# One factor of the short convolution: from two column products to a seven-product block behind the other factor's

## The chip, the cores and the metric

The kernel runs on one core of one Trainium2 chip. The metric is the device time of one execution in microseconds (us), as the median of several runs. TensorE (PE in the profile, its weight loads PEld) multiplies, VectorE (DVE) and ScalarE (ACT) work elementwise, GpSimd (POOL) and SyncE (SP) here mostly issue DMAs.

## What is computed

One decoder layer on 256 tokens of width 2048, all in float32: half a SwiGLU feed-forward, a token mixer, half a second feed-forward, a final norm. The mixer's part of the reference, where all five pieces come from one projection `w_in` (2048 x 5120):

```python
z = rms_norm(x, mix_norm[l]) @ w_in[l]
# lru_x, lru_gate, sc_b, sc_c, sc_x: 1024 columns of z each
xc = causal_depthwise_conv(lru_x, lru_conv_w[l]) + lru_conv_b[l]
h = rg_lru(xc, lru_w_a[l], lru_b_a[l], lru_w_i[l], lru_b_i[l], lru_lambda[l])
y_lru = h * jax.nn.gelu(lru_gate, approximate=True)
y_sc = sc_b * causal_depthwise_conv(sc_c * sc_x, sc_conv_w[l])
y = jnp.concatenate([rms_norm(y_lru, lru_out_norm[l]), rms_norm(y_sc, sc_out_norm[l])], axis=-1)
x = x + y @ w_out[l]
```

The text calls `sc_c` C and `sc_x` X. They are only needed as their product.

## The kernel before

Every float32 operand is split into a high part (float32r, "hi") and a low part (the rest, "lo"); hi x hi, hi x lo and lo x hi are summed in PSUM. A weight tile of 512 rows x 512 columns, a *unit*, is loaded by SP as 1 MB (`raw`), cast by ScalarE in two halves (`hi`), and its low part made by VectorE (raw minus hi). A pair of hi and lo buffers is reused when TensorE has used it; outside the blocks there are two pairs and three rooms for raw.

The input projection has two forms. `columns` makes 512 columns of z, transposed (columns on the partitions): four units, each with 16 matmuls of a 128 x 128 weight piece against 512 elements (hi and lo of x side by side) and 16 against 256. Its result comes in two halves that ScalarE copies and VectorE adds. After each unit `pump` takes deferred work from a queue until a budget is used up, and it is by `defer` that the convolutions, gates, scans and GELUs of the eight heads are spread over the following units.

`seven` makes 1024 columns at once, with tokens on the partitions, as 2 x 2 blocks: of the 16 products of 512 rows, 512 columns and 128 tokens, the 8 over rows 0 to 1023 become 7 products of sums (Strassen's scheme), so 15 remain, each of 12 matmuls against 512 elements. The four weight blocks of rows 0 to 1023 are `w11`, `w12`, `w21`, `w22`; those of the rest are `b2`, `b3`, `a2`, `a3`. The order of the work is: product 0 (on w11), product 4 (on w11 + w12), b2 twice, product 5 (w22 added), b3 twice, product 6 (w12 + w22), product 2 (w22), a2 twice, product 3 (on w11 + w21, with w11 as the earlier sums left it), a3 twice, product 1 (w21). The sums are VectorE's, made in place in w11, except `w12 += w22`, which is a DMA that accumulates, issued by POOL. `w11` and `w12` lie in rooms of their own, the other six take turns in the three raw rooms, so w21 is loaded where w22 was. Inputs of products are named `_p`, the plain ones `_x`. Snapshots of PSUM (`snap`) are combined in `done`, and `turn` transposes the finished 512 columns back.

Before, only C was made by `seven` (in `sc_c`, between the first and the second call of `columns`); X by two calls of `columns` (`sc_x`) among seven: lru_x 1, gate 0, X 0, gate 1, X 1, b 0, b 1. After them comes the output projection (`product`, tiles `o`), whose rows 0 to 1023 are the eight heads (`yT`).

A scheduler orders the instructions of each engine when the program is built, by the order in which the code is written and by when it takes operands to be ready. At run time each engine goes through its list in order, and so do POOL's and SP's queues.

Of the kernel before, what the change touches and what calls it, by code (L numbers as in the profile page):

```python
# [176 lines left out]
def hybrid_block(ctx: ExitStack, tc: tile.TileContext, a: dict, out: bass.AP):  # L177
# [10 lines left out]
    def defer(cost, fn):  # L188
        pending.append((cost, fn))
# [437 lines left out]
    def whole(u):  # L627
        return [(UK * u, UK)]
# [4 lines left out]
    def quad(tile):  # L633
        return tile.rearrange("p (j c) -> p j c", j=UK)

    def seven(w, rows, cols, sf, xs, name, keep, done, between=None, early=False, own=None, factor=None):

# [1117 lines left out]
    with ExitStack() as mixer:  # L1755
# [128 lines left out]
        def lru_x(ps, half):  # L1884
            qs = range(4 * half, 4 * half + 4)
            for f, q in enumerate(qs):
                z = tmp("zx", q, S + 3, bufs=4)
                nc.gpsimd.memset(z[:, :3], 0.0)
                b = halves(ps[f], f"x{q}")
                dve.tensor_tensor(b, ps[f][:, :S], b, op=ALU.add)  # L1890
                dve.tensor_tensor(z[:, 3:], b, bc, op=ALU.mult)
                zx[q] = z
            ts[half] = tmp("T", half, 4 * S)
            for q in qs:
                hs[q] = ts[half][:, (q % 4) * S : (q % 4 + 1) * S]
                defer(1.2, lambda q=q: conv_lru(q))
                defer(0.8, lambda q=q: gates(q))
            defer(3.1, lambda: inverse(half))
            defer(2.8, lambda: drive(half))
            for q in qs:  # L1900
                defer(0.6, lambda q=q: scan(q))

        def lru_gate(ps, half):
            for f in range(4):
# [26 lines left out]
            last()  # L1931
            part(2)

        def sc_c(between):
            r2 = work.tile([P, NT], F32, tag="r2", name="r2")
            dve.tensor_tensor(r2, nm.r, nm.r, op=ALU.mult)
            rt = [r2[:, t : t + 1] for t in range(NT)]
            r2n = work.tile([P, NT], F32, tag="r2n", name="r2n")
            dve.tensor_scalar(r2n, r2, -1.0, None, op0=ALU.mult)
            nt = [r2n[:, t : t + 1] for t in range(NT)]  # L1940
            room = [tmp(tag, "snap", 4 * S, bufs=1) for tag in "vd"]
            free = [b[:, o : o + CW] for b in room for o in (0, CW)]
            z = {}

            def turn(n):
                for f in range(0, 4, 2):
                    pt = bank(f"pt_c{n}_{f}")
                    for i in range(2):
                        for t in range(NT):
                            o = i * S + t * P  # L1950
                            pe.transpose(pt[:, o : o + P], z[t, n][:, (f + i) * P : (f + i + 1) * P], ident)
                    for i in range(2):
                        q = 4 * (1 - n) + f + i
                        c = tmp("cc", q, S + 2, bufs=8)
                        nc.gpsimd.memset(c[:, :2], 0.0)
                        act.copy(c[:, 2:], pt[:, i * S : (i + 1) * S])
                        cc[q] = c

            def done(t, n, ps, tiles):
                for p in tiles[1:]:  # L1960
                    dve.tensor_tensor(tiles[0], tiles[0], p, op=ALU.add)
                    free.append(p)
                if tiles:
                    z[t, n] = tiles[0]
                    dve.scalar_tensor_tensor(z[t, n], ps, rt[t], z[t, n], op0=ALU.mult, op1=ALU.add)
                else:
                    z[t, n] = free.pop()
                    act.activation(z[t, n], ps, AF.Copy, scale=rt[t])
                if (t, n) == (1, 0):
                    turn(1)  # L1970

            c0 = 3 * (D // 2)
            extra.append(bigs)
            turn_of["split"] = 0
            seven(
                w_in, (whole(0), whole(1)), (c0 + CW, c0), si, [of_unit(u, nm.xT[u]) for u in (2, 3)], "in_c", lambda name: free.pop(0), done,
                lambda i: between() if i == 1 else None,
                factor={"s1": rt[0], "s5": rt[1], "u2": nt[0], "u3": nt[1]},
            )
# [12 lines left out]
        def sc_b(ps, half):  # L1992
            if any(4 * half + f not in ys for f in range(4)):
# [7 lines left out]
                defer(0.8, lambda q=q, y=y: finish(y, NH + q, vec["sc_out_norm"][:, q : q + 1], 1, q == 0))  # L2001

        order = [
            (lru_x, 0, 0), (lru_x, 0, 1), (lru_gate, 1, 0), (sc_x, 4, 0), (lru_gate, 1, 1), (sc_x, 4, 1),
            (sc_b, 2, 0), (sc_b, 2, 1),
        ]
        operands()
        behind = None
        for i, (use, part, half) in enumerate(order):
            ps = columns(w_in, part * (D // 2) + half * CW, nm.xT, f"in_{part}_{half}", behind)  # L2010
            behind = None
            if i == 0:
# [5 lines left out]
                behind = sc_c(lambda: use(ps, half))  # L2018
# [196 lines left out]
```

## Time and profile before

| | |
|---|---|
| median of 3 runs | 1715.32 us (1714.56 to 1715.74) |
| the profiled execution | 1716.32 us, of which its span (first to last instruction) is 1714.5 |
| granted TensorE clock | 0.999 |
| input projection in the span | 698.3 to 927.8 us |
| block of C | 723.0 to 764.9 us |
| output projection | 927.8 us onwards |

A timeline row gives the start, the duration, the engine, the line, the operation, out<-in, the shapes and how many alike follow each other; behind it, in brackets, idle time of the engine before it and what ended it. Most rows say L43, the line of a helper, so tiles tell them apart. A windows row gives the stretch, its length, and for PE, PEld, DVE, ACT and POOL the busy time with the number of instructions, then the granted clock, the share of DMA time and GB/s. A group row ends with busy us and mean ns of one, and the idle time before. A waits row gives us in total, times, and the longest.

### The profile page before, as it was taken

Reading aid. Unit: us, or ns where it says so; the run is one execution under the profiler, and the core shown is the slowest. Engines: PE = TensorE matmul, PEld = TensorE weight load, DVE = VectorE, ACT = ScalarE, POOL = GpSimd, SP = SyncE. Lnnn points to the kernel's source line nnn. Section 1 sums busy time; section 2 is a strip of 40 time slices with the busy share of each in tenths; the row PEclk is TensorE's granted clock in tenths of the full one; section 3 lists DMA queues with packets and bytes.
Section 4 is the critical chain, followed back from the end, with each engine's and each line's share of the span. In section 5 each row is a group of like instructions: output and inputs, shape, how many; then the busy total and the mean of one; then the engine's idle time right before and its main releaser. Section 6 shows DMA issues by size and latency. Waiting matters only on the chain.

```text
span 1714.5 us, 20422 instructions
## 1 busy us (share of the span) xinstructions
PE 1701.4 (99%) x7889; PEld 1416.4 (83%) x7889; DVE 1549.2 (90%) x1346; ACT 1109.7 (65%) x1360; POOL 56.0 (3%) x90
## 2 busy tenths in 40 slices
PE   9999999999999999999999999999999999999997
PEld 8888888888888888888888888888888888888886
DVE  7989999999899998887897888899899998999997
ACT  7666576665666667667865666656666665666665
POOL 0010000000000000000000000000000000000000
PEclk9999999999999999999999999999999999999999
DMA  8776877769877768755556674675777878877774
GB/s 283 235 220 197 263 246 227 232 212 265 284 227 227 258 199 255 245 175 180 175 195 206 210 259 148 220 243 173 233 251 233 266 239 243 270 226 240 230 245 148
DMA packets 183315, 389.39 MB, mean 227 GB/s; under 512 B 7605, under 2 KB 10545, under 8 KB 177969
## 3 DMA queue, kind: packets, MB, share of 16 engines
q1 hardware_dynamic: 174656, 340.81, 56.8%
q0 software_dynamic: 8384, 46.21, 13.9%
q8 instruction: 62, 1.02, 0.2%
q10 hardware_dynamic: 176, 1.06, 0.2%
q14 instruction: 37, 0.30, 0.0%
HBM read 339.82 MB, written 2.10 MB: 199 GB/s over the span
## 4 chain that ended last, share of the span: by engine, by line
PE 96%; DVE 2%; ACT 1%; issue 0%; DMA 0%; DVEq 0%; ACTq 0%
PE ps_in L43 10%; PE ps_g_a L43 10%; PE ps_u_a L43 10%; PE ps_d_a L43 9%; PE ps_g_c L43 6%; PE ps_u_c L43 6%; PE ps_d_c L43 5%; PE ps_g_d L43 4%; PE ps_u_d L43 4%; PE ps_d_d L43 4%; PE ps_d_e L43 4%; PE ps_d L43 4%; PE ps_o L43 3%; PE ps_g_e L43 3%; PE ps_u_e L43 2%; PE ps_g L43 2%
## 5 line engine op out<-in xcount | busy, mean ns | idle before, releaser
L43 ACT CAST hi_g_p<-raw_g_w 128x1024 fp32r<-128x1024 f32 (+1 forms) x112 | 139.2, 1263 | 97.4 <-DVE raw_g_w L43 34.5
L43 ACT CAST hi_u_p<-raw_u_w 128x1024 fp32r<-128x1024 f32 x112 | 138.2, 1262 | 66.5 <-PE ps_u_a L43 19.1
L43 DVE TENSOR_TENSOR lo_g_p<-raw_g_w,hi_g_p 128x2560 fp32r<-128x2560 f32 (+2 forms) x72 | 159.9, 2228 | 15.7 <-ACT hi_g_p L43 8.8
L43 DVE TENSOR_TENSOR lo_u_p<-raw_u_w,hi_u_p 128x2560 fp32r<-128x2560 f32 (+2 forms) x72 | 159.1, 2228 | 9.4 <-ACT hi_u_p L43 6.7
L43 ACT CAST hi_d_p<-raw_d_w 128x1024 fp32r<-128x1024 f32 x112 | 112.7, 1047 | 53.7 <-DVE raw_d_w L43 22.3
L43 DVE TENSOR_TENSOR lo_d_p<-raw_d_w,hi_d_p 128x2048 fp32r<-128x2048 f32 (+1 forms) x72 | 129.4, 1812 | 5.8 <-ACT hi_d_p L43 5.5
L43 PE MATMUL ps_in<-xT_nm,hi_in 128*128 128x512 f32 x512 | 123.5, 392 | 0.0
L43 PEld LDWEIGHTS ps_in<-xT_nm,hi_in 128*128 128x128 f32 x512 | 94.0, 188 | 18.7 <-ACT tha L43 0.5
L43 DVE TENSOR_TENSOR lo_in<-raw_in,hi_in 128x2048 fp32r<-128x2048 f32 x32 | 73.3, 2291 | 20.4 <-ACT hi_in L43 20.0
L43 ACT CAST hi_in<-raw_in 128x1024 fp32r<-128x1024 f32 x64 | 64.0, 1045 | 32.2 <-PE ps_in L43 18.4
L43 ACT CAST hi_d_x<-raw_d_x 128x1024 fp32r<-128x1024 f32 x64 | 64.3, 1046 | 19.3 <-PE ps_d_c L43 8.1
L43 DVE TENSOR_TENSOR lo_d_x<-raw_d_x,hi_d_x 128x2048 fp32r<-128x2048 f32 x32 | 72.7, 2286 | 1.5 <-ACT hi_d_x L43 1.3
L43 DVE TENSOR_TENSOR raw_u_w<-raw_u_w,raw_u_w 128x1024 f32<-128x1024 f32 (+2 forms) x40 | 69.4, 1757 | 3.8 <-DMA raw_u_w<-in_ffn_w_up_dram 3.0
L43 DVE TENSOR_TENSOR raw_g_w<-raw_g_w,raw_g_w 128x1024 f32<-128x1024 f32 (+2 forms) x40 | 69.5, 1755 | 1.4 <-DMA raw_g_w<-in_ffn_w_gate_dram 0.8
L43 PEld LDWEIGHTS ps_in<-xT_nm,lo_in 128*128 128x128 f32 x512 | 65.6, 191 | 2.5
L43 PE MATMUL ps_in<-xT_nm,lo_in 128*128 128x256 f32 x512 | 66.4, 283 | 0.0
L43 DVE TENSOR_TENSOR lo_g_x<-raw_g_x,hi_g_x 128x1536 fp32r<-128x1536 f32 x32 | 56.1, 1754 | 3.7 <-ACT hi_g_x L43 3.6
L43 PE MATMUL ps_u_a<-hi_u_p,x 128*128 128x512 f32 x224 | 57.1, 391 | 0.0
L43 ACT CAST hi_g_x<-raw_g_x 128x1536 fp32r<-128x1536 f32 x32 | 47.2, 1475 | 15.1 <-DMA raw_g_x<-in_ffn_w_gate_dram 11.3
L43 PE MATMUL ps_g_a<-hi_g_p,x 128*128 128x512 f32 x224 | 56.6, 389 | 0.0
L43 DVE TENSOR_TENSOR lo_u_x<-raw_u_x,hi_u_x 128x1536 fp32r<-128x1536 f32 x32 | 56.1, 1753 | 0.0
L43 ACT CAST hi_u_x<-raw_u_x 128x1536 fp32r<-128x1536 f32 x32 | 47.3, 1477 | 12.4 <-PE ps_u_c L43 7.0
(513 smaller groups left out, 4248.1 us busy)
## 6 DMA issues: line engine op xcount, KB each, us to landing
raw_g_w<-in_ffn_w_gate_dram SPq DMA_DIRECT2D x32, 1024.0 KB, 6.6
raw_u_w<-in_ffn_w_up_dram SPq DMA_DIRECT2D x32, 1024.0 KB, 6.4
raw_d_w<-in_ffn_w_down_dram SPq DMA_DIRECT2D x32, 1024.0 KB, 5.4
raw_d_x<-in_ffn_w_down_dram SPq DMA_DIRECT2D x32, 1024.0 KB, 6.9
raw_in<-in_w_in_dram SPq DMA_DIRECT2D x32, 1024.0 KB, 5.0
raw_d<-in_ffn_w_down_dram SPq DMA_DIRECT2D x24, 1024.0 KB, 5.2
raw_g_x<-in_ffn_w_gate_dram SPq DMA_DIRECT2D x32, 768.0 KB, 7.8
raw_u_x<-in_ffn_w_up_dram SPq DMA_DIRECT2D x32, 768.0 KB, 8.5
```

The costliest lines, as they stand in the source:

```text
L43: ins = getattr(self.engine, name)(*args, **kwargs)
```

## The change

X is made by `seven` too, right behind C: `sc_c` becomes `token_block`, called for C and then for X by `sc_cx`. C's last transposes are written behind X's first product, and X's transposed columns are multiplied into C's (`times_x`) straight from PSUM. In both blocks `w11 += w21` becomes an accumulating DMA of POOL (`moved=True`). The two calls of `columns` for X go, the budget of `pump` in `columns` goes from 1.9 to 2.9, and the short convolution of the second four column tiles is deferred by `lru_x`.

```diff
-            pump(1.9)
+            pump(2.9)
...
         product_of(0, w11, a, True)
+        if moved:
+            between("first product")
         dve.tensor_tensor(w11, w12, w11, op=ALU.add)
         nc.gpsimd.dma_start(w12, w22, accum_op=ALU.add)
...
         product_of(5, w11, a)
+        if moved:
+            nc.gpsimd.dma_start(w11, w21, accum_op=ALU.add)
...
-        dve.tensor_tensor(w11, w21, w11, op=ALU.add)
+        if not moved:
+            dve.tensor_tensor(w11, w21, w11, op=ALU.add)
         product_of(3, w11, a, end=own is not None or not two)
...
             for q in qs:
                 defer(0.6, lambda q=q: scan(q))
+            for q in qs if half else ():
+                defer(1.5, lambda q=q: conv_short(q))
...
-        def sc_x(ps, half):
-            for f in range(4):
-                q = 4 * half + f
...
+            def times_x(q, pt):
                 c = cc[q][:, 2:]
-                b = halves(ps[f], f"sx{q}")
-                dve.tensor_tensor(b, ps[f][:, :S], b, op=ALU.add)
-                dve.tensor_tensor(c, b, c, op=ALU.mult)
-                defer(1.5, lambda q=q: conv_short(q))
+                dve.tensor_tensor(c, pt, c, op=ALU.mult)
+                if q < 4:
+                    defer(1.5, lambda: conv_short(q))
+
+            rest = token_block(3, "in_c", lambda i: between() if i == 1 else None, as_c, (rt, nt))
+            return token_block(4, "in_x", lambda i: rest() if i == "first product" else None, times_x)
...
         order = [
-            (lru_x, 0, 0), (lru_x, 0, 1), (lru_gate, 1, 0), (sc_x, 4, 0), (lru_gate, 1, 1), (sc_x, 4, 1),
-            (sc_b, 2, 0), (sc_b, 2, 1),
+            (lru_x, 0, 0), (lru_x, 0, 1), (lru_gate, 1, 0), (lru_gate, 1, 1), (sc_b, 2, 0), (sc_b, 2, 1),
         ]
```

How this moves instructions, in the order in which each engine has them. Numbers in names are the program's own; brackets name the semaphores that are waited for (DMASW: a DMA of POOL, DMAHW: one of SP).

First, VectorE at the end of the block of C, before (here 5631 is w11, 5643 is w21, `lo_in_c_p_5856` is product 3's low part, `lo_in_c_p_5925` product 1's):

```order
L43 TENSOR_TENSOR d_snap<-d_snap,v_snap 128x512 [waits Activation_49]
L43 TENSOR_TENSOR raw_in_c_5631<-raw_in_c_5643,raw_in_c_5631 128x2048 [waits DMAHW2_49]
L43 SCALAR_TENSOR_TENSOR d_snap<-ps_in_c_e,r_5621,d_snap 128x512 [waits DVE_49]
L43 SCALAR_TENSOR_TENSOR d_snap<-ps_in_c_c,r_5621,d_snap 128x512 [waits PE_49]
L43 TENSOR_TENSOR lo_in_c_x_5873<-raw_in_c_5645,hi_in_c_x_5872 128x2048 [waits DMAHW1_49,Activation_49]
L43 TENSOR_TENSOR lo_in_c_p_5856<-raw_in_c_5631,hi_in_c_p_5855 128x2048 [waits DVE_49,Activation_49]
L43 TENSOR_TENSOR lo_in_c_p_5925<-raw_in_c_5643,hi_in_c_p_5924 128x2048 [waits PE_49,Activation_49]
```

and in the changed program:

```order
L43 TENSOR_TENSOR d_snap_in_c<-d_snap_in_c,v_snap_in_c 128x512 [waits Activation_49]
L43 SCALAR_TENSOR_TENSOR xc_6406<-zx_5726,cols_conv,xc_6406 128x256 [waits DVE_49]
L43 SCALAR_TENSOR_TENSOR d_snap_in_c<-ps_in_c_e,r_5621,d_snap_in_c 128x512 [waits DVE_49]
L43 SCALAR_TENSOR_TENSOR xc_6406<-zx_5726,cols_conv,xc_6406 128x256 [waits DVE_49]
L43 SCALAR_TENSOR_TENSOR d_snap_in_c<-ps_in_c_c,r_5621,d_snap_in_c 128x512 [waits PE_49]
L43 TENSOR_TENSOR lo_in_c_x_5873<-raw_in_c_5645,hi_in_c_x_5872 128x2048 [waits DMAHW1_49,Activation_49]
L43 TENSOR_TENSOR lo_in_c_p_5856<-raw_in_c_5631,hi_in_c_p_5855 128x2048 [waits DMASW6_49,Activation_49]
L43 TENSOR_TENSOR lo_in_c_p_5925<-raw_in_c_5643,hi_in_c_p_5924 128x2048 [waits DMAHW2_49,PE_49,Activation_49]
```

The sum `raw_in_c_5631<-raw_in_c_5643,raw_in_c_5631` is gone from VectorE, product 3's low part waits for a DMA of POOL instead, two rows of a head's convolution (`xc_6406`) have moved in, and X's first low part follows directly.

Second, POOL's queue from the accumulating DMA of C on (`zx` are the padded inputs of the heads' convolutions, `raw_o_q` belongs to the output projection), before:

```order
L682 DMA raw_in_c_5633<-raw_in_c_5637 128x2048 [waits DMAHW6_49,DMAHW4_49,DVE_49]
L1888 MEMSET zx_6232 128x3 [waits DVE_49,Activation_49]
L1888 MEMSET zx_6238 128x3 [waits DVE_49,Activation_49]
L1888 MEMSET zx_6244 128x3 [waits DVE_49,Activation_49]
L1888 MEMSET zx_6250 128x3 [waits DVE_49,Activation_49]
L682 DMA raw_o_q_8008<-raw_o_q_8012 128x2048 [waits DMAHW1_49,DMASW4_49,DMAHW3_49,DVE_49,Activation_49]
```

and in the changed program:

```order
L684 DMA raw_in_c_5633<-raw_in_c_5637 128x2048 [waits DMAHW6_49,DMAHW4_49,DVE_49]
L1893 MEMSET zx_6539 128x3 [waits DVE_49,Activation_49]
L1893 MEMSET zx_6545 128x3 [waits DVE_49,Activation_49]
L711 DMA raw_in_c_5631<-raw_in_c_5643 128x2048 [waits DMAHW2_49,Activation_49]
L1893 MEMSET zx_6551 128x3 [waits DVE_49,Pool_49]
L684 DMA raw_in_x_5950<-raw_in_x_5954 128x2048 [waits DMAHW6_49,DMASW6_49,DMAHW7_49,DVE_49,Activation_49]
L711 DMA raw_in_x_5948<-raw_in_x_5960 128x2048 [waits DMAHW2_49,DVE_49,PE_49]
L1893 MEMSET zx_6557 128x3 [waits DVE_49,Activation_49]
```

Three DMAs have come in: C's `w11 += w21` behind the second MEMSET of `zx`, X's `w12 += w22` behind the third, and X's `w11 += w21` directly behind that.

Third, VectorE in the calls of `columns`, at the recurrence of the second four heads (`T`, `d`, `v`; the rows named `lo_in` are the units' low parts), before:

```order
L43 SCALAR_TENSOR_TENSOR y_e_6764<-T_6256,d_6553 128x1024
L43 TENSOR_TENSOR g_3_7172<-g_3_7172,g_6444 128x256
L43 SCALAR_TENSOR_TENSOR d_6553<-y_e_6764,d_6553 128x1024
L43 TENSOR_SCALAR T_6256<-T_6256 128x1024
L43 SCALAR_TENSOR_TENSOR v_6552<-v_6552,d_6553 128x1024
L43 TENSOR_TENSOR lo_in_1_3_6853<-raw_in_1_3_6850,hi_in_1_3_6852 128x2048
L43 TENSOR_TENSOR v_6552<-v_6552,T_6256 128x1024
L43 TENSOR_SCALAR d_6553<-d_6553 128x1024
L43 SCALAR_TENSOR_TENSOR g_3_7172<-g_3_7172,g_6444 128x256
L43 SCALAR_TENSOR_TENSOR T_6256<-d_6553,v_6552 128x256
L43 TENSOR_TENSOR lo_in_1_0_6917<-raw_in_1_0_6914,hi_in_1_0_6916 128x2048
L43 SCALAR_TENSOR_TENSOR T_6256<-d_6553,v_6552 128x256 x3
```

and in the changed program:

```order
L43 SCALAR_TENSOR_TENSOR d_6829<-y_e_6981,d_6829 128x1024
L43 TENSOR_SCALAR T_6563<-T_6563 128x1024
L43 SCALAR_TENSOR_TENSOR v_6828<-v_6828,d_6829 128x1024
L43 TENSOR_TENSOR g_7028<-ps_in_1_0_6770,half_g_7029 128x256
L43 TENSOR_SCALAR d_6829<-d_6829 128x1024
L43 TENSOR_TENSOR g_7028<-g_7028,bc_nm 128x256
L43 TENSOR_TENSOR g_7033<-ps_in_1_1_6771,half_g_7034 128x256
L43 TENSOR_TENSOR v_6828<-v_6828,T_6563 128x1024
L43 TENSOR_TENSOR g_7033<-g_7033,bc_nm 128x256
L43 SCALAR_TENSOR_TENSOR T_6563<-d_6829,v_6828 128x256 x3
L43 TENSOR_TENSOR lo_in_0_1_7097<-raw_in_0_1_7094,hi_in_0_1_7096 128x2048
```

Two low parts stood among the rows of the recurrence between `d<-y_e` and the scans, and now none stands there until three scans are done; the stretch now lies in the first call for b (`lo_in_0_1_7097` is its second unit), where before it lay in the second call for the gate.

More of the change, by code (lines that the diff above doesn't have):

```diff
@@ L634, in quad, with seven @@
         return tile.rearrange("p (j c) -> p j c", j=UK)
-    def seven(w, rows, cols, sf, xs, name, keep, done, between=None, early=False, own=None, factor=None):
+    def seven(w, rows, cols, sf, xs, name, keep, done, between=None, early=False, own=None, factor=None, moved=False):
         apart = {}
@@ L1932, in operands, with token_block @@
             part(2)
[L1934 to L1941, printed above, removed]
+        def token_block(part, name, between, use, factor=None):
+            rt, nt = factor or (None, None)
+            room = [tmp(tag, f"snap_{name}", 4 * S, bufs=1) for tag in "vd"]
             free = [b[:, o : o + CW] for b in room for o in (0, CW)]
@@ L1946, in turn @@
                 for f in range(0, 4, 2):
-                    pt = bank(f"pt_c{n}_{f}")
+                    pt = bank(f"pt_{name}{n}_{f}")
                     for i in range(2):
@@ L1952, in turn @@
                     for i in range(2):
[L1953 to L1957, printed above, removed]
+                        use(4 * (1 - n) + f + i, pt[:, i * S : (i + 1) * S])
             def done(t, n, ps, tiles):
@@ L1962, in done @@
                     free.append(p)
-                if tiles:
-                    z[t, n] = tiles[0]
+                z[t, n] = tiles[0] if tiles else free.pop()
+                if not tiles:
+                    act.activation(z[t, n], ps, AF.Copy, scale=rt[t] if rt else 1.0)
+                elif rt:
                     dve.scalar_tensor_tensor(z[t, n], ps, rt[t], z[t, n], op0=ALU.mult, op1=ALU.add)
                 else:
-                    z[t, n] = free.pop()
-                    act.activation(z[t, n], ps, AF.Copy, scale=rt[t])
+                    dve.tensor_tensor(z[t, n], ps, z[t, n], op=ALU.add)
                 if (t, n) == (1, 0):
                     turn(1)
-            c0 = 3 * (D // 2)
+            c0 = part * (D // 2)
             extra.append(bigs)
@@ L1975, in sc_c @@
             seven(
-                w_in, (whole(0), whole(1)), (c0 + CW, c0), si, [of_unit(u, nm.xT[u]) for u in (2, 3)], "in_c", lambda name: free.pop(0), done,
-                lambda i: between() if i == 1 else None,
-                factor={"s1": rt[0], "s5": rt[1], "u2": nt[0], "u3": nt[1]},
+                w_in, (whole(0), whole(1)), (c0 + CW, c0), si, [of_unit(u, nm.xT[u]) for u in (2, 3)], name,
+                lambda name: free.pop(0), done, between,
+                factor=factor and {"s1": rt[0], "s5": rt[1], "u2": nt[0], "u3": nt[1]}, moved=True,
             )
@@ L2017, in hybrid_block @@
                 bc = nm.bc
-                behind = sc_c(lambda: use(ps, half))
+                behind = sc_cx(lambda: use(ps, half))
                 gate_weights("a", a["lru_w_a"][0])
```

11 lines of the change are left out of this document (added).

## The prediction

> **What bounds the kernel now.** I read the page first: busy shares, then the chain that ended last.
>
> ```profile
> PE 1701.4 (99%) x7889; PEld 1416.4 (83%) x7889; DVE 1549.2 (90%) x1346; ACT 1109.7 (65%) x1360; POOL 56.0 (3%) x90
> PE 96%; DVE 2%; ACT 1%; issue 0%; DMA 0%; DVEq 0%; ACTq 0%
> ```
>
> TensorE sets the end almost everywhere. Then I asked for the waits of its weight loads (PEld) in the input projection, 698 to 973 us, and for the two stretches that the change rewrites.
>
> ```profile
> PEld ps_in L43 <- ACT tha L43: 0.5, 2, 0.3
> PEld pt_nm L43 <- DVE xT_nm L43: 0.4, 1, 0.4
> PEld ps_in_c_a L43 <- DVE lo_in_c_p L43: 0.3, 1, 0.3
> PEld ps_in L43 <- ACT thi L43: 0.2, 1, 0.2
> ...
> 723.04:764.86 41.82, 41.82 (x191) 34.46 (x190) 36.60 (x37) 28.59 (x41) 0.55 (x4) 1.00 0.52 152
> 764.86:927.81 162.95, 162.95 (x953) 144.25 (x952) 135.61 (x199) 116.47 (x202) 0.10 (x1) 1.00 0.58 190
> ```
>
> Four waits, 1.4 us in all: there is nothing to win but TensorE instructions, and every wait that is added shows in the time. VectorE is 88% busy in the block (36.60 of 41.82) and 83% behind it (135.61 of 162.95).
>
> **What TensorE saves.** The timeline of weight loads prices both forms: a unit of `columns` (16 loads `hi_in`, 16 `lo_in`) and the block of C.
>
> ```profile
> 723.04 1.69 PEld L43 LDWEIGHTS ps_in_c_a<-hi_in_c_p,xT_nm 128*128 128x128 f32 x8
> 761.24 1.02 PEld L43 LDWEIGHTS pt_c<-ident,d_snap 128*128 128x128 f32 x8
> 762.24 1.68 PEld L43 LDWEIGHTS ps_in_c_d<-hi_in_c_p,xT_nm 128*128 128x128 f32 x8
> 764.86 3.59 PEld L43 LDWEIGHTS ps_in<-xT_nm,hi_in 128*128 128x128 f32 x16
> 770.52 0.90 PEld L43 LDWEIGHTS pt_c<-ident,v_snap 128*128 128x128 f32 x8
> 771.38 0.42 PEld L43 LDWEIGHTS pgate_a<-xs,gate_a 128*128 128x128 f32 x3
> 771.73 0.42 PEld L43 LDWEIGHTS pgate_i<-xs,gate_i 128*128 128x128 f32 x3
> 772.09 3.51 PEld L43 LDWEIGHTS ps_in<-xT_nm,hi_in 128*128 128x128 f32 x16
> 844.31 3.51 PEld L43 LDWEIGHTS ps_in<-xT_nm,hi_in 128*128 128x128 f32 x16
> 927.81 3.51 PEld L43 LDWEIGHTS ps_o<-hi_o,yT 128*128 128x128 f32 x16
> ```
>
> Between 844.31 and 927.81 lie 15 units and nothing else: 5.57 us each. The two `columns` calls of X are eight units, 44.5 us. The block of C lasts from 723.04 to 764.86, 41.8 us; without eight transposes (762.24 - 761.24 = 1.0) and the 0.3 us wait it is 40.5 for 15 products of 12 matmuls, 2.7 each. X's block is 40.5 + 1.0 + 0.86 (the other eight transposes, 771.38 - 770.52) = 42.4. **Term 1: -2.1 us.** The projection's granted clock is 1.00 in the windows' rows, so no clock term.
>
> **What the moved sum costs.** `w11 += w21` leaves VectorE and becomes a DMA of POOL's queue, in both blocks. Before, in the block of C:
>
> ```profile
> DMA to landing us min/median/max: 5.0/5.0/5.0
> 735.93 0.76 PEld L43 LDWEIGHTS ps_in_c_a<-lo_in_c_p,xis 128*128 128x128 f32 x4 [0.30 <-DVE lo_in_c_p L43]
> 736.73 1.80 PEld L43 LDWEIGHTS ps_in_c_e<-hi_in_c_x,xT_nm 128*128 128x128 f32 x8
> 738.82 2.29 DVE L43 TENSOR_TENSOR lo_in_c_p<-raw_in_c,hi_in_c_p 128x2048 fp32r<-128x2048 f32 x1
> 741.14 0.37 SPq L43 DMA_DIRECT2D raw_in_c<-in_w_in_dram  x1
> 746.68 2.29 DVE L43 TENSOR_TENSOR raw_in_c<-raw_in_c,raw_in_c 128x2048 f32<-128x2048 f32 x1
> 749.11 1.99 ACT L43 CAST hi_in_c_p<-raw_in_c 128x1024 fp32r<-128x1024 f32 x2
> 753.08 1.77 PEld L43 LDWEIGHTS ps_in_c_a<-hi_in_c_p,xT_nm 128*128 128x128 f32 x8
> 754.90 0.87 PEld L43 LDWEIGHTS ps_in_c_a<-lo_in_c_p,xT_nm 128*128 128x128 f32 x4
> raw_in_c<-raw_in_c POOLq DMA_DIRECT2D x1, 1024.0 KB, 8.0
> raw_o_q<-raw_o_q POOLq DMA_DIRECT2D x1, 1024.0 KB, 7.0
> raw_d_w<-raw_d_w POOLq DMA_DIRECT2D x16, 1024.0 KB, 7.3
> raw_u_w<-raw_u_w POOLq DMA_DIRECT2D x8, 1024.0 KB, 9.7
> ```
>
> w21 goes into the room that w22 had, so its load waits for the low part of w22 (738.82 + 2.29 = 741.1). It is issued at 741.14 and lands 5.0 later (the first row is for this one load), at 746.1. The sum then took 2.3, the cast began at 749.1, and TensorE came for it at 753.08: 4 us of room. The same sum by DMA took 8.0 the one time that this block did it, 7.0 to 9.7 elsewhere. With 8.0: landed 754.2, first half cast (half of 1.99, and a hop) 755.3, TensorE starts at 755.4 instead of 753.1: 2.3 late. Its low part then needs the second cast and 2.29 of VectorE, until 758.6, while TensorE has eight loads of the high part (1.8) and two that the new order puts between (0.45), until 757.7: 0.9 more. **Term 2: +3.2 us in C**; at 7.0 it is +2.2, at 9.7 +4.9.
>
> X's block has the same chain: from the end of product 5 (736.73) to product 3 (753.08) TensorE has 16.3 us of work, and the room of w22 again comes free 4.4 after that end. Fewer other loads run then, so I take 7.5 for its DMA, and only one load stands between the parts: **term 3: +2.9 us in X** (2.4 to 5.1).
>
> Behind the waiting cast stand, on ScalarE, the casts of product 1's input and of X's first two inputs, and on VectorE their low parts. TensorE asks for product 1's input at 762.24, 6.4 us after product 3 ends (754.90 + 0.9), and a cast with its low part takes 4.3: no second wait follows in C.
>
> **What X's block adds to the other engines** I count at nothing. VectorE gets eleven low parts and two sums of 2.29, four snapshot sums and four products with C:
>
> ```profile
> 749.54 0.74 DVE L43 SCALAR_TENSOR_TENSOR d_snap<-ps_in_c_c,r,d_snap 128x512 f32<-128x512 f32 x1
> ```
>
> 13 x 2.29 + 4 x 0.74 + 4 x 0.42 = 34.4 us, under TensorE's 42.4; C's block held 36.6 with a single wait of 0.3. The cover is that the order fills neither block's idle VectorE time with head work beyond the first three convolutions; without it, each us over 42.4 would be one of time. The first input of X needs buffers that C's last products give back, one product earlier than TensorE asks. ScalarE casts eleven inputs at 2.0, 22 us. The loads stay eight of 1 MB; three accumulating DMAs of 1 MB come on top, with DMA at 0.52 of its share in C's block (the windows' row).
>
> Another cover counted at nothing is POOL's queue. The new DMA stands behind two MEMSETs of `zx`.
>
> ```profile
> 742.82 0.10 POOL L1888 MEMSET zx<- 128x3 f32 x1 [0.29 <-ACT hi_in_c_x L43]
> ```
>
> That second MEMSET went at 742.8, 3.3 us ahead of the landing of w21; were it later than 746.1, each us would be one of stall. X's first DMA stands behind a third MEMSET, which waits for the convolution of head 2; that convolution moves ahead into the block of C (the first listing), so I count nothing.
>
> **What is crowded behind.** Seven `columns` calls followed the blocks, now five: 20 units, eight pairs of gate products (772.09 - 771.38 = 0.71) and 0.86 of transposes, 118 us. Their VectorE work:
>
> ```profile
> L43 DVE TENSOR_TENSOR lo_in<-raw_in,hi_in 128x2048 fp32r<-128x2048 f32 x28 | 64.2, 2291 | 17.8 <-ACT hi_in L43 17.4 <-PE pgate_a L43 0.4
> L43 DVE TENSOR_TENSOR cc<-half_sx,cc 128x256 f32<-128x256 f32 x8 | 3.0, 422 | 0.0
> L43 DVE TENSOR_TENSOR half_sx<-ps_in,half_sx 128x256 f32<-128x256 f32 x8 | 3.0, 418 | 0.0
> L43 DVE SCALAR_TENSOR_TENSOR y_e<-T,d 128x1024 f32<-128x1024 f32 x2 | 2.4, 1224 | 0.8 <-ACT d L43 0.8
> L43 DVE TENSOR_TENSOR_SCAN T<-d,v 128x256 f32<-128x256 f32 x8 | 5.1, 679 | 0.0
> ```
>
> 135.6 less eight low parts (8 x 2.29 = 18.3), the halves of X (3.0) and half of the products with C (1.5) is about 113 us in 118: 96% busy instead of 83%. The printed order shows where it bunches: between the low parts of b's first two units stand four operations of 1024 elements (1.22 each), three scans (0.68), two scalar ones and eight small ones, with the low part about 12 us, against 11.1 for two units; before, such a batch was cut by low parts. A low part can be made at most about 7 us ahead (two pairs of buffers), which covers one such batch, not two. The same holds for the last heads' GELU, on which the first output product's second half waits. I price these places by hand at 0 to 1.5 us each, three of them: **term 4: +1.9 us**, from 0 (all inside the slack) to 6 (VectorE and ScalarE wait for each other at every head). The `pump(2.9)` itself only hands this work out faster.
>
> **Sum.** -2.1 + 3.2 + 2.9 + 1.9 = **+5.9 us**. The span is 1714.5 in an execution of 1716.32, 1.0 above the median 1715.32, so the sum goes to the median: **1721.2 us**.
>
> **Rivals.** (a) *The sum lands in time*, not slower: if landing takes under about 5.5 us, C's cast is at TensorE by 753.1 and terms 2 and 3 vanish; with term 4 at 0 the time is 1715.3 - 2.1 = 1713.2, up to 1715. For it: a plain 1 MB load took 5.0. Against it: the four groups of accumulating DMAs quoted above have medians of 7.0 to 9.7. The Trainium skill, "DMA: Bandwidth & Descriptors", section "Anatomy of one DMA — SWDGE (gpsimd) path", fits a DMA issued from GpSimd as 2.0 us plus the bytes at 436 GB/s, 4.4 us for 1 MB; by that figure, an estimate from the page, this rival would win, but the fit is of loads, and the trace's 8.0 for this very sum disagrees. Chance 0.13.
> (b) *VectorE becomes the bound behind the blocks*: a backlog that 5% of slack doesn't repay goes on into the output product. Term 4 is then 6 to 10: 1727, to 1729. For it: 96% busy, and ScalarE's tanh chains alternate with VectorE in order. Against it: 17.4 us of VectorE's idle time before were only waits for the cast of a unit that was early. Chance 0.14.
> (c) *The change doesn't move what it says*: POOL held by a MEMSET, so that the DMAs start late and both blocks stall further; 1 to 5 us more, about 1725. The MEMSET's 3.3 us of lead speaks against it. Chance 0.04.
>
> **Numbers.** Forecast 0.69, with its own range 1717.8 to 1726.2 (both sums at 7.0 and term 4 at 0: -2.1 + 2.2 + 2.4 = +2.5; both at 9.7 and term 4 at 3: -2.1 + 4.9 + 5.1 + 3 = +10.9). The range reaches down towards (a) and up into (b): 1716.5 to 1727.5. This kernel's measurement tells no difference under 0.2%, 3.4 us. TensorE's saving alone is 0.12%, so faster needs a gain that no row shows: 0.04. Same holds (a) and the low end of the forecast: 0.20. Slower: 0.76.
>
> **What would show it.** In the changed trace: 15 products of X near 40.5 us plus waits; a wait of PEld `ps_in_c_a` and `ps_in_x_a` for the cast of product 3's input, 2 us each, and a shorter one for its low part; POOL rows of line 711 with a landing of 7 to 8; VectorE over 93% busy in the five calls. It is wrong if those landings are under 5.5 us, or if the waits of the last five calls add up to more than the two blocks'.

## The result, and the profile after

The changed kernel takes 1723.0 us, the median of 5 runs (1720.92 to 1724.85), against 1715.56 us (1714.56 to 1716.24) before. The ratio is 1.0041, with a 95% interval from 1.003 to 1.0053: slower by 5 to 9 us. The forecast was 1721.2 in a range of 1716.5 to 1727.5.

The profiled execution took 1720.92 us and spans 1719.1, 4.6 us more than the span before. The page first: TensorE has less to do (1698.8 us against 1701.4), and the chain that ended last could be followed back only to 755 us, product 3 of C's block (its shares add up to 56%).

```profile
PE 1698.8 (99%) x7829; PEld 1410.8 (82%) x7829; DVE 1557.0 (91%) x1346; ACT 1115.7 (65%) x1363; POOL 58.6 (3%) x93
PE 51%; DVE 3%; ACT 1%; DMA 1%; issue 0%; DVEq 0%; ACTq 0%; POOLq 0%
```

The windows of the three stretches (C's block, X's block, the five remaining calls of `columns`); the columns are length, busy time and instructions of PE, PEld, DVE, ACT and POOL, the granted clock, the DMA share and GB/s.

```profile
721.36:767.35 45.99, 42.44 (x191) 34.26 (x190) 36.34 (x36) 28.29 (x40) 1.44 (x5) 1.00 0.74 224
767.35:813.81 46.46, 43.67 (x197) 35.00 (x196) 31.55 (x22) 25.90 (x32) 1.73 (x2) 1.00 0.59 164
813.81:933.85 120.04, 118.81 (x698) 105.11 (x696) 107.36 (x164) 91.17 (x158) 0.10 (x1) 1.00 0.55 187
```

C's block took 41.82 us before and takes 45.99. X's block takes 46.46 where two `columns` calls took 44.5. Together the three last 212.49 us against 204.77, so that the projection lost 7.7 us. The whole span lost less because its other parts differ between executions: the projection began at 696.6 us instead of 698.3, though nothing ahead of it had changed, and reached the block 24.7 us later in both (in all profiles of this study the block began between 720.91 and 723.78), and from the first load of `ps_o_q`, the seven-product block of the output product, to the end it took 739.9 us instead of 741.3. The lengths of the three stretches are therefore the better measure, and the difference of the medians, 7.4 us, agrees with them.

What lengthened them is in the waits of PEld between 690 and 990 us (total, times, longest):

```profile
PEld ps_in_c_a L43 <- ACT hi_in_c_p L43: 3.5, 2, 3.3
PEld ps_in_x_a L43 <- ACT hi_in_x_p L43: 2.4, 2, 2.2
PEld ps_in_c_a L43 <- DVE lo_in_c_p L43: 1.4, 2, 1.1
PEld ps_in_x_a L43 <- DVE lo_in_x_p L43: 1.3, 1, 1.3
PEld pgate_a L43 <- DVE xs L43: 0.9, 1, 0.9
PEld ps_in L43 <- DVE half_b L43: 0.8, 1, 0.8
```

The first four are product 3 of the two blocks, whose weight sum the change gave to POOL (but for 0.30 us in the third row, the wait of product 5 that was there before). Its chain in the timeline, C's block first: the DMA is issued, ScalarE casts what has landed, VectorE makes the low part, and TensorE waits for each.

```profile
745.10 0.89 POOL L711 DMA_DIRECT2D raw_in_c<-raw_in_c  x1 [3.86 <-DMA raw_in_c<-in_w_in_dram]
753.55 3.89 ACT L43 CAST hi_in_c_p<-raw_in_c 128x1024 fp32r<-128x1024 f32 x4 [6.04 <-DMA raw_in_c<-raw_in_c]
754.65 0.76 PEld L43 LDWEIGHTS ps_in_c_a<-hi_in_c_p,xT_nm 128*128 128x128 f32 x4 [3.29 <-ACT hi_in_c_p L43]
755.58 4.49 DVE L43 TENSOR_TENSOR lo_in_c_p<-raw_in_c,hi_in_c_p 128x2048 fp32r<-128x2048 f32 x2 [5.75 <-ACT hi_in_c_p L43]
757.93 0.76 PEld L43 LDWEIGHTS ps_in_c_a<-lo_in_c_p,xT_nm 128*128 128x128 f32 x4 [1.10 <-DVE lo_in_c_p L43]
792.32 0.86 POOL L711 DMA_DIRECT2D raw_in_x<-raw_in_x  x1 [21.30 <-DMA raw_in_x<-in_w_in_dram]
799.78 3.89 ACT L43 CAST hi_in_x_p<-raw_in_x 128x1024 fp32r<-128x1024 f32 x4 [4.95 <-DMA raw_in_x<-raw_in_x]
800.87 0.76 PEld L43 LDWEIGHTS ps_in_x_a<-hi_in_x_p,xT_nm 128*128 128x128 f32 x4 [2.16 <-ACT hi_in_x_p L43]
804.15 0.76 PEld L43 LDWEIGHTS ps_in_x_a<-lo_in_x_p,xT_nm 128*128 128x128 f32 x4 [1.34 <-DVE lo_in_x_p L43]
```

The releasers stand in the brackets: each step is held by the one above it, and POOL by the load of w21, not by a MEMSET. From issue to cast are 8.4 us in C (745.10 to 753.55) and 7.4 in X (792.32 to 799.78).

The chain that ended last, listed in order of time (start, length, what), runs through X's block along this very path; before, it was TensorE for 96%:

```profile
784.47 2.30 DVE lo_in_x_p L43
786.78 4.92 DMA raw_in_x<-in_w_in_dram
...
791.73 0.04 POOLq L711
791.77 0.55 issue
792.32 7.43 DMA raw_in_x<-raw_in_x
...
800.73 1.05 ACT hi_in_x_p L43
801.80 2.30 DVE lo_in_x_p L43
...
804.15 3.02 PE ps_in_x_a L43 x12
```

The low part of w22 frees the room, w21 is loaded into it, the sum runs, then cast, low part and product 3: six links, of which 12.4 us are the two DMAs. Between the landing of w21 and the start of the sum lie another 0.6 us, most of it listed as issue on POOL.

### The profile page after: what moved, and what is told of

Its sections match the earlier page's. It is cut to its first block, busy times and chain, and to the rows that moved or that the text cites. A ratio compares the mean times of both kernels' runs of the same rounds, so it can differ in the third digit from the quotient of the medians.

```text
span 1719.1 us, 20321 instructions
## 1 busy us (share of the span) xinstructions
PE 1698.8 (99%) x7829; PEld 1410.8 (82%) x7829; DVE 1557.0 (91%) x1346; ACT 1115.7 (65%) x1363; POOL 58.6 (3%) x93
## 4 chain that ended last, share of the span: by engine, by line
PE 51%; DVE 3%; ACT 1%; DMA 1%; issue 0%; DVEq 0%; ACTq 0%; POOLq 0%
PE ps_g_a L43 5%; PE ps_u_a L43 5%; PE ps_d_a L43 5%; PE ps_in L43 4%; PE ps_u_c L43 3%; PE ps_g_c L43 3%; PE ps_o L43 3%; PE ps_d_c L43 2%; PE ps_u_d L43 2%; PE ps_g_d L43 2%; PE ps_d_e L43 2%; PE ps_d_d L43 2%; PE ps_d L43 2%; PE ps_u L43 1%; PE ps_u_e L43 1%; PE ps_g L43 1%
## 5 line engine op out<-in xcount | busy, mean ns | idle before, releaser
L43 PE MATMUL ps_in<-xT_nm,hi_in 128*128 128x512 f32 x384 | 93.0, 392 | 0.6 <-DVE half_b L43 0.6
L43 PEld LDWEIGHTS ps_in<-xT_nm,hi_in 128*128 128x128 f32 x384 | 70.6, 188 | 14.3 <-DVE half_b L43 0.8
L43 ACT CAST hi_in<-raw_in 128x1024 fp32r<-128x1024 f32 x48 | 48.2, 1045 | 22.5 <-PE ps_in L43 12.6
L43 DVE TENSOR_TENSOR lo_in<-raw_in,hi_in 128x2048 fp32r<-128x2048 f32 x24 | 55.0, 2295 | 7.8 <-ACT hi_in L43 7.8
L43 PEld LDWEIGHTS ps_in<-xT_nm,lo_in 128*128 128x128 f32 x384 | 49.3, 191 | 2.2 <-DVE lo_in L43 0.4
L43 PE MATMUL ps_in<-xT_nm,lo_in 128*128 128x256 f32 x384 | 50.1, 283 | 0.0
```

The source lines that it names most:

```text
L43: ins = getattr(self.engine, name)(*args, **kwargs)
```

## The experiments

Eleven runs follow; `e11` is the changed kernel once more. `e1` to `e4` ran side by side, as did `e5` to `e8`, and `e9` with `e10`; each ratio is against the kernel before on the same chip. Lengths of the stretches in us, each from its own profile, with the waits of PEld inside in brackets:

| kernel | C's block | X's block | five calls | all three | median us | ratio (95%) |
|---|---|---|---|---|---|---|
| before | 41.82 (0.3) | in columns | 162.95 (0.7) with X | 204.77 | 1715.56 | |
| changed | 45.99 (4.9) | 46.46 (4.7) | 120.04 (2.1) | 212.49 | 1723.0 | 1.0041 (1.003 to 1.0053) |
| e1, both sums on VectorE | 41.79 (0.3) | 43.16 (1.0) | 120.03 (2.1) | 204.98 | 1714.93 | 0.9998 (0.9989 to 1.0007) |
| e2, X's sum on VectorE | 46.23 (3.5) | 43.16 (1.0) | 120.02 (2.1) | 209.41 | 1721.52 | 1.0033 (1.002 to 1.0046) |
| e3, before with C's sum by DMA | 45.58 (3.1) | in columns | 162.91 (0.7) with X | 208.49 | 1718.97 | 1.0018 (1.0009 to 1.0027) |
| e4, sums by DMA from DRAM | 41.79 (0.3) | 43.61 (1.4) | 123.68 (4.4) | 209.08 | 1717.73 | 1.0015 (1.0006 to 1.0024) |
| e5, e1 with budget 1.9 | 41.83 (0.3) | 43.18 (1.1) | 118.41 (0.7) | 203.42 | 1721.8 | 1.0038 (1.0025 to 1.0051) |
| e6, before with budget 2.9 | 41.83 (0.3) | in columns | 163.56 (1.2) with X | 205.39 | 1716.23 | 1.0005 (0.9996 to 1.0014) |
| e7, e4 in another order | 41.79 (0.3) | 43.54 (1.3) | 120.02 (2.1) | 205.35 | 1716.35 | 1.0009 (1.0 to 1.0018) |
| e8, w21 in the room of b2 | 45.59 (2.9) | 44.60 (2.8) | 120.51 (2.6) | 210.70 | 1721.72 | 1.0041 (1.0028 to 1.0054) |
| e9, e1 with rising budgets | 41.85 (0.3) | 43.17 (1.0) | 119.38 (1.7) | 204.40 | 1715.05 | 0.9998 (0.9989 to 1.0007) |
| e10, e1 with budget 3.2 | 41.80 (0.3) | 43.18 (1.0) | 124.64 (5.0) | 209.62 | 1720.55 | 1.0034 (1.0022 to 1.0047) |
| e11, changed again | 46.74 (4.3) | 46.61 (4.8) | 120.04 (2.1) | 213.39 | 1724.35 | 1.005 (1.0036 to 1.0064) |

Not every length is waits alone. In C's block of e2, e3, e8 and e11 (mean granted clock 0.96) and in the five calls of e4 and e10 (0.99) TensorE also ran for some us at about half clock, right behind a wait; in the other stretches of the table the clock is 1.00. The last section deals with it.

**e1: both sums back on VectorE.**

```diff
-        if moved:
-            nc.gpsimd.dma_start(w11, w21, accum_op=ALU.add)
...
-        if not moved:
-            dve.tensor_tensor(w11, w21, w11, op=ALU.add)
+        dve.tensor_tensor(w11, w21, w11, op=ALU.add)
```

> The changed kernel with w11 += w21 back on VectorE in both blocks; the rest of the change stays. Theory (the late landing is the main cost): the waits for product 3's input in the two blocks, 3.29 + 0.19 + 1.10 in C and 2.16 + 0.19 + 1.34 in X in the changed kernel's trace, go away; of those 8.3 us at most 2 come back where VectorE takes the two sums of 2.29 us again. Time 1714.7 to 1717, that is the same as before within 0.2%; ps_in_c_a and ps_in_x_a wait under 2 us together. Rival (crowding on VectorE is the cost, the sum's DMA relieved it): 1722 or more, and the waits move to lo_in_x_p and to the five calls behind, over 5 us there.

All four waits for product 3 are gone, and the time is that of before. Its windows:

```profile
721.08:762.87 41.79, 41.79 (x190) 34.46 (x189) 38.43 (x37) 28.29 (x40) 0.55 (x4) 1.00 0.64 206
762.87:806.03 43.16, 43.02 (x198) 35.22 (x197) 33.38 (x23) 25.31 (x31) 0.89 (x1) 1.00 0.55 166
806.03:926.06 120.03, 118.79 (x698) 105.03 (x697) 107.45 (x164) 91.83 (x158) 0.10 (x1) 1.00 0.56 187
```

VectorE carries 2.1 us more in C and 1.8 more in X than in the changed kernel, and costs nothing by it: the rival, that the DMA relieved VectorE, falls. The two moved sums are worth 4.20 us in C and 3.30 in X.

**e2: only X's sum on VectorE** (the DMA line under `if name == "in_c":`, the VectorE line under its opposite).

> The changed kernel with the moved sum as a DMA in C's block only, on VectorE in X's. Theory: X's 3.7 us go, C's stay: 1719 to 1720.5; the waits of ps_in_c_a are about 4.5 us, those of ps_in_x_a under 1.5. Rival (X's waits come from a DMA that C's delay pushes together, or from VectorE): X waits as long, 1722 to 1724.

X's waits fell from 4.7 to 1.0 and its block by 3.30 us; so far as the theory says. But C's block did not get cheaper, and the median is 1 us over what was expected. C's wait for the low part is gone, the block's waits are 3.5 us instead of 4.9, and yet its length is 46.23 us. The row shows why: eight weight loads took 3.03 us where they take 1.77, and the window behind the wait shows the granted clock.

```profile
755.49 3.03 PEld L43 LDWEIGHTS ps_in_c_a<-hi_in_c_p,xT_nm 128*128 128x128 f32 x8 [3.21 <-ACT hi_in_c_p L43]
```

```profile
755.40:758.50 3.10, 3.00 (x7) 2.43 (x8) 2.08 (x1) 2.88 (x4) 0.00 (x0) 0.51 1.05 401
```

More on that clock stands in the last section.

**e3: the kernel before, with C's sum by DMA and nothing else.**

```diff
         product_of(5, w11, a)
+        if name == "in_c":
+            nc.gpsimd.dma_start(w11, w21, accum_op=ALU.add)
...
-        dve.tensor_tensor(w11, w21, w11, op=ALU.add)
+        if name != "in_c":
+            dve.tensor_tensor(w11, w21, w11, op=ALU.add)
```

> The kernel before with one edit: in C's block w11 += w21 is an accumulating DMA; X stays in columns. Theory: the stall of C's block comes from this edit alone, 3 to 5 us, and nothing gives it back later: 1718.5 to 1720.5; C's block lasts 45 to 46.5 us. Rival (the stall needs the crowding and the new order of work around the block): under 1716.5, C's block under 43 us.

As expected: C's block is 3.76 us longer, the 162.9 us behind it are as before, and the ratio is worth 1.5 to 4.6 us. Waits make 2.8 us of the 3.76; the rest comes with a half clock behind them (0.50 from 757.5 to 760.5 us). The stall needs neither X's block nor the new order; nothing gives it back.

**e4: the same sums by DMA, but from DRAM.**

```diff
         if moved:
-            nc.gpsimd.dma_start(w11, w21, accum_op=ALU.add)
+            k, n = r1[0]
+            src = w[k * P : (k + n) * P, cols[0] : cols[0] + CW].rearrange("(j p) c -> p j c", p=P)
+            nc.gpsimd.dma_start(w11, src, accum_op=ALU.add)
```

> The changed kernel with the moved sum still an accumulating DMA of POOL's queue, but one that reads w21 from DRAM instead of from the room in which its load lands. It needs no landing of w21 and no room, so that it can be issued once product 5's low part is made, some 12 us earlier, ahead of the MEMSETs. Theory (not the DMA's length but its place at the end of a chain room-load-sum-cast costs the time): both waits for product 3's input are under 0.5 us though the DMA itself takes 7 us or more; with TensorE's saving of 2.1 us and 1 to 2 us behind the blocks 1713.5 to 1716. Rival (accumulating DMAs of 1 MB slow the other loads, or are themselves too slow from DRAM): waits over 2 us for hi_in_c_p or for a plain load, 1719 or more.

In the blocks the theory holds: POOL issues the DMA at 734.16 us instead of 745.10, it takes 8.4 us as in the changed kernel, and no wait for product 3 is left.

```profile
734.16 1.34 POOL L713 DMA_DIRECT2D raw_in_c<-in_w_in_dram  x1 [12.99 <-DVE lo_in_c_p L43]
```

The time is 1.7 us over the expected range all the same, for a new wait stands at the first unit behind X's block (rows of PEld, DVE and ACT):

```profile
807.63 1.05 ACT L43 CAST gate_i<-rawgate_i 128x1024 fp32r<-128x1024 f32 x1 [2.85 <-DMA rawgate_i<-in_lru_w_i_dram]
808.71 1.23 DVE L43 TENSOR_TENSOR gate_i<-rawgate_i,gate_i 128x1024 fp32r<-128x1024 f32 x1 [3.75 <-ACT gate_i L43]
809.85 2.28 DVE L43 TENSOR_TENSOR lo_in<-raw_in,hi_in 128x2048 fp32r<-128x2048 f32 x1
812.18 2.79 PEld L43 LDWEIGHTS ps_in<-xT_nm,lo_in 128*128 128x128 f32 x16 [2.29 <-DVE lo_in L43]
```

TensorE waits for `lo_in`, whose input had long been cast; on VectorE it stands behind `gate_i`, whose load now goes out behind two of the calls' loads on SP's queue where in e1 it was one (one place, not the two that the next expectation names). **e7** puts that right: w21 is gathered after a3, and the gate weights i are loaded and cast behind the next call's first unit.

```diff
-                behind = sc_cx(lambda: use(ps, half))
+                rest = sc_cx(lambda: use(ps, half))
                 gate_weights("a", a["lru_w_a"][0])
-                gate_weights("i", a["lru_w_i"][0])
+                behind = lambda: (rest(), gate_weights("i", a["lru_w_i"][0]))
```

> The run named e4 (sums by DMA from DRAM, 1717.73) with two things put in another order: w21 is loaded after a3, so that the rooms are taken in the order in which the products use them, and the gate weights i are loaded and cast behind the first unit of the next call. Theory (e4 lost 3.7 us at the first unit behind X's block, since its low part stood on VectorE behind the low part of gate_i, whose load had slipped two places on SP's queue; the accumulating DMAs from DRAM cost nothing): the five calls last 120 to 120.6 us instead of 123.68, and the time is 1713.5 to 1715. Rival (the two extra megabytes from DRAM themselves make the loads behind late): the five calls stay over 122 us, 1717 or more.

The five calls are back at 120.02 us, so the DMAs from DRAM took nothing from them (which of the two edits did it was not separated). The median, 1716.35, is 1.4 us above the expected range; by its stretches (205.35) the kernel is that of e1 within 0.4 us, and nothing is won by freeing VectorE of 4.6 us.

**e8: the chain shortened at its head.** w21 is gathered ahead of a2, so that it takes the room of b2 and a2 that of w22; the sum stays room to room.

```diff
-        a2, w21 = get(xs[0][0], 0, "short0"), get(r1, 0, "tall2")
+        if moved:
+            w21, a2 = get(r1, 0, "tall2"), get(xs[0][0], 0, "short0")
+        else:
+            a2, w21 = get(xs[0][0], 0, "short0"), get(r1, 0, "tall2")
```

> The changed kernel with one thing put in another order: w21 is loaded before a2, into the room of b2, which comes free some 10 us earlier than that of w22; the sum stays the same accumulating DMA from room to room. Theory (the chain room of w22 - load 5 - sum 8 - cast sets the stall, not the DMA by itself): the DMA is issued near 737 us instead of 745 and, at 7.5 to 8.5 us as before, lands by 746: the waits of ps_in_c_a and ps_in_x_a for hi_in_c_p and hi_in_x_p fall from 5.7 us in all to under 0.6; a2 comes later and may cost up to 1 us in each block; 1714.5 to 1717. Rival (an accumulating DMA costs time by itself, through ports or the other loads): 1719 or more.

The DMA goes out at 736.23 and both waits for product 3's cast are gone, as the theory says. But the time, 1721.72, lies where the rival had it and can't be told from the changed kernel's: the expectation allowed a2 at most 1 us per block, and its waits are 2.6 in C and 2.1 in X. Rows of POOL, DVE and PEld in C's block, and the window behind the wait:

```profile
736.23 0.89 POOL L714 DMA_DIRECT2D raw_in_c<-raw_in_c  x1 [12.94 <-DVE lo_in_c_p L43]
746.96 2.29 DVE L43 TENSOR_TENSOR lo_in_c_p<-raw_in_c,hi_in_c_p 128x2048 fp32r<-128x2048 f32 x1
751.21 4.48 DVE L43 TENSOR_TENSOR lo_in_c_x<-raw_in_c,hi_in_c_x 128x2048 fp32r<-128x2048 f32 x2
753.54 1.16 PEld L43 LDWEIGHTS ps_in_c_d<-lo_in_c_x,xT_nm 128*128 128x128 f32 x4 [2.26 <-DVE lo_in_c_x L43]
```

```profile
753.50:756.00 2.50, 2.46 (x6) 1.95 (x7) 2.19 (x1) 1.99 (x2) 0.00 (x0) 0.56 0.51 141
```

The cast of a2, now in the late room, held TensorE for only 0.35 us in C. The rest is the order of work on VectorE: product 3's low part (746.96), early now, and three snapshot sums stand ahead of a2's low part, though TensorE needs a2 first. The stall of the sum, 4.6 us of waits in C and 3.7 in X, is gone, and the new order makes another of a little over half its size. X's block shows the difference, 44.60 us against 46.46; C's block hides it, since behind its wait TensorE ran at about half clock (the last row), which the changed kernel's profile doesn't have.

**e5 and e6: the budget of head work** (`pump(2.9)` to `pump(1.9)` in e1; `pump(1.9)` to `pump(2.9)` in the kernel before).

> The changed kernel with both sums on VectorE, as in the run named e1 (1714.93 us; five calls 120.03 us with waits of 2.1), and the budget of head work per unit back from 2.9 to 1.9. Theory (term 4: what two calls fewer leave has to be done in five, and the budget only sets how soon): head work is not done when the calls end, it is flushed there in one piece, and VectorE's low parts behind wait for it: three to eight us more, 1718 to 1723, with the wait in the sixth part of the projection or ahead of the output product. Rival (the batches that 2.9 makes are the cause of the 2.1 us of waits in the five calls): these waits fall under 1 us, 1713.5 or less.

> The kernel before with the budget 2.9 in place of 1.9 and nothing else. Theory (VectorE has room there, 83% busy, so handing out sooner costs little and wins nothing): 1715 to 1716.5, waits of PEld behind C's block between 0.7 and 2 us. Rival (the larger batches by themselves make the three waits of the five calls, xs 0.93, lo_in 0.35, half_b 0.83): 1717 or more, and the same three waits appear.

In e5 both theories came true in part. The three waits of the five calls are gone (118.41 us, 0.7 of waits): it is the budget that makes them, by larger batches or by more work in the calls (VectorE has 102.31 us there instead of 107.45), which e5 doesn't tell apart. And the output product's part ahead of `ps_o_q` pays 7.25 us for the work that is left over (52.61 instead of 45.36); it waits for `yT`, which the flushed heads make:

```profile
937.32 0.30 PEld L43 LDWEIGHTS ps_o<-hi_o,yT 128*128 128x128 f32 x2 [3.60 <-ACT yT L43]
926.58:979.19 52.61, 49.05 (x211) 39.45 (x210) 49.42 (x83) 37.23 (x71) 0.87 (x1) 0.94 0.57 200
```

Only half of the 7.25 us is idle time. PE is busy for 49.05 us where e1 has it busy for 45.32 in the same part: 3.7 us of the price are matmuls at half clock behind that wait.

In e6 the waits behind C's block rise from 0.7 to 1.2 us only, in other places; the larger batches are harmless while VectorE has 27 us of room in 163.

**e9 and e10: other budgets in e1** (2.4, 2.4, 2.9, 3.4, 3.4 in the five calls; 3.2 in all).

> The run named e1 (sums on VectorE, budget 2.9: five calls 120.03 us, waits 2.1) with budgets of 2.4, 2.4, 2.9, 3.4 and 3.4 in the five calls. Theory (the waits come from batches that are too large early, the flush of e5 from work left at the end): smaller batches first and larger ones last take the wait of xs away and leave no flush: calls 118.5 to 119.5, 1713.5 to 1714.8, and at best 1 us under before, which the intervals won't tell from no change. Rival (larger batches at the end stall the output product's inputs): 1716 or more.

> The run named e1 with the budget 3.2 in all five calls. Theory (batches set the waits): as many waits or more than at 2.9, 2.1 to 5 us in the calls, no flush: 1715 to 1718. Rival (a larger budget only moves work to an emptier place): waits under 1.5 us, under 1714.5.

With rising budgets the calls take 119.38 us, as expected, and the time, 1715.05, is that of before and 0.25 us above the expected range. With 3.2 the waits grow to 5.0 us, one of them for ScalarE, which has to cast `xs` behind such a batch:

```profile
860.71 0.19 PEld L43 LDWEIGHTS pgate_a<-xs,gate_a 128*128 128x128 f32 x1 [3.10 <-ACT xs L43]
```

The median, 1720.55, is 2.6 us above the expected range, which held no term for the clock: it was 0.68 from 860.7 to 863.0 us and 0.76 from there to 867, and PE is busy for 120.42 us in the calls instead of 118.79.

**e11: the changed kernel once more.**

> The changed kernel once more, nothing edited. Its profiled execution took 1720.92 us, its other four runs 1721.18 to 1724.85, at mean granted clocks of 0.999 to 0.997. Theory (a stall of over 2 us is sometimes followed by some 3.4 us at a granted clock of 0.5, as in the runs named e2, e3, e4, e5, e8 and e10; the profiled execution of the changed kernel escaped it): the new profile shows a granted clock near 0.5 right behind the wait of 3.3 us in C's block or that of 2.2 us in X's, the block that has it is 1.2 to 1.7 us longer than the 45.99 or 46.46 us seen before, and the time is 1721 to 1725. Rival (the spread is of other origin, the FFNs or the opening): no clock under 0.9 between 721 and 980 us, and blocks of 46.0 and 46.5 us again, with a median over 1722 us all the same.

It took 1724.35 us, the median of 5 (1721.9 to 1725.44), ratio 1.005 (1.0036 to 1.0064). Its profile, of span 1723.3, has the clock dip in C's block and none in X's; C's block is 46.74 us, 0.75 longer, less than was expected, since the slow stretch covers part of the wait for the low part (0.42 instead of 1.10). Of the 4.2 us between the two spans that dip explains 0.8; 1.9 lie ahead of the block (it began at 723.25) and 1.4 behind 980 us. The rival is right for the larger share.

None of the kernels is faster than the one before by more than the intervals show. The change without the moved sums (e1, e9) equals it.

## Why the prediction was right, and where it was off

The forecast held, by the steps that it gave:

- **What bounds.** Right. Before, TensorE's weight loads waited 1.0 us in the three stretches; now 11.7, and the stretches are longer by 7.7.
- **Term 1, -2.1 us.** X's block without its waits takes 43.16 - 1.01 = 42.15 us in e1 (42.4 was worked out). What was counted at nothing beside it, waits of product 4 for its low part and of two snapshots, is 1.0 us. Net -1.3.
- **Term 2, +3.2 us in C.** The mechanism is right row by row; the size is +4.2. The landing took 8.4 us instead of 8.0. The rest is a step that the sum put at nothing, the one from the landing of w21 to the start of POOL's DMA. The load of w21 was issued 18.1 us after the block's start and took 5.0, as before; but the DMA started at 23.7 us, 0.6 behind the landing, where the sum had it start at once (23.1).
- **Term 3, +2.9 us in X.** It is +3.3, with a landing of 7.4 where 7.5 was taken. The same step accounts for the missing 0.4 us: X's chain lists 0.55 of issue ahead of the DMA.
- **Term 4, +1.9 us.** 162.95 less X's 44.5 is 118.45; the five calls take 120.04: +1.6, in three waits. That the number is near 1.9 is partly luck, for only the smallest wait is one that the forecast describes: 0.35 us for the low part behind the recurrence, in the first call for b. The heads' GELU costs 0.82, but in the second call for b, not in the output product; `half_b` stands on VectorE behind a row that waits 2.8 us for ScalarE. The largest, 0.93 for `xs` in the second call for the gate, wasn't named. VectorE is 89% busy in the five calls (107.36 of 120.04), not 96%, so what costs is not a lack of room but what stands in front of the row that TensorE needs. And the sentence that `pump(2.9)` only hands the work out faster missed that the budget sets this price: 0.7 us of waits at 1.9, 2.1 at 2.9, 5.0 at 3.2, against 7.25 us (waits and half clock together) in the output product at 1.9.
- **The sum.** -1.3 + 4.2 + 3.3 + 1.6 = +7.8 against +5.9. Three of the four terms came out worse than forecast and one slightly better, so the number doesn't owe its place in the range to errors that cancel.
- **Rival (a), the sum lands in time,** falls by the landings of 8.4 and 7.4 us. The Trainium skill's fit in "DMA: Bandwidth & Descriptors", section "Anatomy of one DMA — SWDGE (gpsimd) path", from which 4.4 us was estimated, does not hold for these DMAs, neither from room to room nor from DRAM (8.4 in e4). That section of the Trainium skill gives the fit per DMA; that it is of loads, as the prediction has it, isn't said there. Still, e4 shows the other half of that rival's idea: with the same 8.4 us, issued 10.5 us earlier in C's block, the waits are gone.
- **Rival (b), a backlog that reaches the output product,** did not happen: the output product's part ahead of `ps_o_q` takes 45.32 us against 45.36. e5 shows what it would have cost. **Rival (c)**, POOL held by a MEMSET, did not happen either: the second one of C's block ran at 741.1, 4 us ahead of the DMA.
- **The signs.** The waits for product 3's cast are there (3.3 us in C and 2.2 in X, where 2 each were named), each with a shorter one for the low part, and the waits of the five calls (2.1) stay below those of the blocks (9.6). VectorE over 93% busy in the calls did not come.

## What to carry to other kernels

An operation moved from a busy engine to a DMA is paid for by its latency, 2.3 us on VectorE against 7.4 to 8.4 here, and some 0.6 between its release and its start; look at what releases it and what takes it next, and move it only where both leave that much room. If the stall sits behind a load that waits for a room, a source that needs no room (DRAM) takes the stall away, while another order of the rooms here handed over half of it to the next tile. And where fewer units must cover the same side work, the size of the batches is a quantity to be tuned: by their ratios to the kernel before, which e1 equals, the smaller budget cost 6.5 us and the larger 5.8, part of it by the clock.

## What the runs showed of the hardware

Ten waits of PEld in these profiles were longer than 2 us. Behind seven of them the granted clock fell to about 0.5: in C's block of e2, e3, e8 and e11, in the calls of e4 and e10, and in the output product of e5. Behind three it did not: both of the changed kernel's, and X's in e11. The wait at 812.18 in e4 was 2.29 us, the one in C's block of e11 3.39; windows of the stretch right behind each:

```profile
813.00:816.40 3.40, 3.40 (x19) 3.40 (x18) 2.17 (x2) 1.33 (x2) 0.00 (x0) 0.51 1.05 396
```

```profile
758.00:761.00 3.00, 3.00 (x9) 2.11 (x8) 3.00 (x2) 2.49 (x4) 0.00 (x0) 0.50 0.78 271
```

In e4 it lasts some 3.4 us and costs about half of that: PE is busy for 120.58 us in the five calls instead of e1's 118.79, and the calls are 3.65 us longer, of which the wait is only 2.29. In e5 the clock is 0.50 for twice as long, from 938.8 to 945.6 us. The changed kernel's profiled execution, with a wait of 3.29 us at the same place as e11's, shows none; this is its window behind the wait:

```profile
754.60:757.90 3.30, 2.60 (x10) 1.72 (x10) 2.32 (x2) 2.84 (x3) 0.00 (x0) 1.00 1.05 401
```

The Trainium skill, "TensorE: Matmul & The Clock Gate", section "What's actually happening", describes a gate that halves TensorE's clock after an idle window of about 3.4 us, in windows that run freely and don't start anew with the kernel. The 3.4 us at half clock, twice that in e5, and that the same wait brings them on in one execution and not in another, agree with such windows. The same page of the Trainium skill, section "Why this matters for your kernels", warns of idle gaps of over 3 us between matmuls; here waits of 2.25 us (in e3) to 2.29 us were enough, in which PE itself was idle for 1.83 to 1.86 us, and the measurement decides. In these runs a stall of 2 to 4 us thus came, in some executions and not in others, with 1.3 us (e11 against the changed kernel's other profile) to 3.7 us (e5 against e1) more busy time of PE for the same matmuls.
